# Prelude of a hybrid transformer block: first modulation in column halves, with low-rank products of half the rows between them

## The chip, the cores and the metric

The kernel runs on one core of a Trainium2 chip. A core has five engines with queues of their own: TensorE (PE in the profile, with its weight loads as PEld), VectorE (DVE), ScalarE (ACT), GpSimd (POOL) and SyncE (SP), which here issues most of the DMA transfers. Each engine works through its queue in order, and the engines wait for each other at semaphores. The metric is the device time of one execution in microseconds (us), less is better; the figure of a kernel is the median of its runs.

## The reference

One block with two mixers (attention with a forget gate, and an RWKV-7 recurrence) and a gated convolutional feed-forward layer, in float32, on 1024 rows of width 1024. The change lies at its very start:

```python
mod = silu(c) @ w_mod + b_mod                       # 1024 -> 6 x 1024
shift1, scale1, gate1, shift2, scale2, gate2 = split(mod, 6)
xn  = x * rsqrt(mean(x * x, -1) + 1e-6) * ln1_g
u   = xn * (1 + scale1) + shift1
proj = u @ w_in
...
xw, xa, xg = p_rwkv[..., 1536:]                     # low-rank inputs, widths 64, 64, 128
w_log = -softplus(-(w0 + tanh(xw) @ w2)) - 0.5
a = sigmoid(a0 + xa @ a2)
g = sigmoid(xg) @ g2
```

All products of u are taken in three parts to keep float32 accuracy: u and a weight are each split into a rounded high part and a low part (high = cast, low = value minus high), and high x high, low x high and high x low are added up in PSUM.

## The kernel before

Everything stands in one function, hybrid_block. PE's instructions stand in the order in which the code calls mm; inside the prelude block (lines 413 to 553) the same holds for SP, DVE and ACT, because manual_schedule names these engines. Outside of it, and for GpSimd, a scheduler places instructions, and it may also slip some of the later ones in between those of the prelude.

The prelude holds u transposed: tile kt (0 to 7) has model columns kt x 128 to kt x 128 + 127 on the partitions, and the rows of x, in two halves of 512 (half 0 and 1), along the free dimension. So a modulation value is one number for each partition of a tile: tile kt needs column kt of m1 (shift) and of A1 (ln1_g times 1 + scale). Its steps are these.

- load_x fetches x as eight tiles xt of 128 rows. square (line 425) sums the squares of a tile on ACT, rms_rstd turns them into 1/rms with Ln and Exp, and norm_x (431) puts 1/rms on the diagonal of a matrix dg on DVE.
- turn (466) multiplies four x tiles with these diagonal matrices on PE: the transposed, normalised x lands in a PSUM tile (two buffers), and ACT copies it into uf[half]. There are 16 turns, half 0 first.
- mod_load (438) fetches w_mod for scale (i = 1) or shift (i = 0) as eight tiles of 128 x 1024; the scale's tiles have four buffers (mw), the shift's take those and the slots of x tiles in turns. mod_add (450) adds sc[kt] times such a tile into acc on DVE, eight times. mod_sum (456) adds up acc over its partitions with 128 x 1 products on PE (mps in the profile) and makes m1 and A1 out of them on DVE. The loop at line 532 does this for the scale and then for the shift; warm (445) puts products into PE's queue whose result nobody reads (idle).
- u_steps (472) scales a tile of uf on DVE, casts it to u_hi on ACT and takes u_lo on DVE; half 0, then half 1. low_part (485) multiplies the tile with the two low-rank weight tiles (w_in tiles 24 and 25, raw_in24 and raw_in25; their casts and subtractions are at lines 538 and 545). Three parts, two weights, eight tiles and two halves make 96 products of 128 x 512 (low in the profile).
- low_out (498) moves the four sums out of PSUM. Behind it the first projection products (ps_rkv, weights through load_w, line 256) start; from there on PE works through the projections, the low-rank second products (zp) and all that follows.

Of the kernel before, what the change touches and what calls it, by code (L numbers as in the profile page):

```python
# [132 lines left out]
def hybrid_block(ctx: ExitStack, tc: tile.TileContext, a, out):  # L133
    nc = tc.nc
# [3 lines left out]
    def mm(o, lhsT, rhs, start, stop, more=False):  # L138

        weave.mm_cost(o, lhsT, rhs)  # L140
        nc.tensor.matmul(o, lhsT, rhs, start=start, stop=stop, skip_group_check=more)  # L141
# [24 lines left out]
    def V(name, i=0, n=1):  # L166
        o, _ = VEC[name]
        return vec[:, o + i : o + i + n]
# [6 lines left out]
    ident, ones = f32(eye_r), f32(C("ones"))  # L175
# [16 lines left out]
    sc = cp.tile([128, 8], F32, name="sc")  # L192
# [16 lines left out]
    m2 = cp.tile([128, 16], F32, name="m2")  # L209
# [105 lines left out]
    A1 = cp.tile([128, 8], F32, name="A1")  # L315
    m1 = cp.tile([128, 16], F32, name="m1")
# [3 lines left out]
    u_hi = upool.tile([128, KT, S], F32R, name="u_hi")  # L320
    u_lo = upool.tile([128, KT, S], F32R, name="u_lo")
# [24 lines left out]
    with ExitStack() as es:  # L346
# [65 lines left out]

        with tc.tile_pool(name="st", bufs=1) as st, tc.tile_pool(name="stp", bufs=2, space=PS) as stp, \
                tc.manual_schedule(engines={mybir.EngineType.SP, mybir.EngineType.DVE, mybir.EngineType.Activation}):
            ssq = st.tile([128, 8], F32, name="ssq")
            rstd = st.tile([128, 8], F32, name="rstd")

            def load_x(half):
                xs = []
                for t in range(half * 4, half * 4 + 4):  # L420
                    xs.append(st.tile([128, D], F32, tag="xt", name=f"xt{t}", bufs=8))
                    nc.sync.dma_start(xs[-1], a["x"][t * 128 : t * 128 + 128, :])
                return xs

            def square(half, xs, js):
                for j in js:
                    t = half * 4 + j
                    nc.scalar.activation(uf[1][:, 6:8, :].rearrange("p k s -> p (k s)"), xs[j], AF.Square,
                                         accum_out=ssq[:, t : t + 1])

            def norm_x(half):

                hs = slice(half * 4, half * 4 + 4)
                rms_rstd(rstd[:, hs], ssq[:, hs])
                for j in range(half * 4, half * 4 + 4):
                    ts(dg[:, j, :], ident, rstd[:, j : j + 1], None, op0=ALU.mult)

            def mod_load(i, tags):
                ws = [st.tile([128, D], F32, tag=tags[kt % len(tags)], name=f"wm{i}{kt}", bufs={"mw": 4, "xt": 8}[tags[kt % len(tags)]])
                      for kt in range(KT)]  # L440
                for kt, w in enumerate(ws):
                    nc.sync.dma_start(w, a["w_mod"][kt * 128 : kt * 128 + 128, i * D : i * D + D])
                return ws, st.tile([128, D], F32, name=f"acc{i}")
# [6 lines left out]
            def mod_add(kt, ws, acc):  # L450
                if kt == 0:
                    ts(acc, ws[kt], sc[:, 0:1], None, op0=ALU.mult)
                else:
                    stt(acc, ws[kt], sc[:, kt : kt + 1], acc, op0=ALU.mult, op1=ALU.add)

            def mod_sum(i, acc):
                for j0 in (0, 4):
                    ps = stp.tile([128, 4], F32, tag="mp", name=f"mps{i}{j0}")
                    for j in range(4):
                        c0 = (j0 + j) * 128  # L460
                        mm(ps[:, j : j + 1], acc[:, c0 : c0 + 128], ones[:, 0:1], start=True, stop=True)
                    tt(m1[:, i * 8 + j0 : i * 8 + j0 + 4], ps, V("b_mod", i * 8 + j0, 4), op=ALU.add)
                    if i == 1:
                        stt(A1[:, j0 : j0 + 4], m1[:, 8 + j0 : 12 + j0], 1.0, V("ln1_g", j0, 4), op0=ALU.add, op1=ALU.mult)
# [7 lines left out]
            def u_steps(half):  # L472

                cs = slice(half * NH, half * NH + NH)
                for kt in range(KT + 1):
                    if kt < KT:
                        x = uf[half][:, kt, :]
                        ts(x, x, A1[:, kt : kt + 1], m1[:, kt : kt + 1], op0=ALU.mult, op1=ALU.add)
                        nc.scalar.copy(u_hi[:, kt, cs], x)
                    if kt > 0:  # L480
                        k = kt - 1
                        tt(u_lo[:, k, cs], uf[half][:, k, :], f32(u_hi[:, k, cs]), op=ALU.subtract)
                        yield k

            def low_part(kt, half, parts):
                for (wh, wl), ps in zip(low, low_ps):
                    for i in parts:
                        w, x = ((wh, u_hi), (wh, u_lo), (wl, u_hi))[i]
                        mm(ps[half], w[:, kt * 128 : kt * 128 + 128], x[:, kt, half * NH : half * NH + NH],
                           start=kt == 0 and i == 0, stop=kt == KT - 1 and i == 2)  # L490
# [18 lines left out]

            dg = xwa.rearrange("p (j s) -> p j s", s=128)  # L510
            idle = pb.tile([128, NH], F32, tag="big", name="idle")
            xs = [load_x(half) for half in range(2)]
            m = [mod_load(1, ("mw",)), None]
            uf = [st.tile([128, KT, NH], F32, name=f"uf{half}") for half in range(2)]
            warm(28)
            for half in range(2):
                square(half, xs[half], range(4))
                norm_x(half)
            for half in range(2):
                for kt in range(KT):  # L520
                    nc.scalar.copy(uf[half][:, kt, :], turn(kt, half, xs[half]))
            m[1] = mod_load(0, ("xt", "mw"))
# [6 lines left out]
            nc.sync.dma_start(g2, a["g2"])  # L529
            for o, c0, w in ((0, CST["mask"][0], 128), (128, CST["reset"][0], 256)):  # L530
                nc.sync.dma_start(cst2[:, o : o + w], a["cst"][:, c0 : c0 + w])
            for i in (1, 0):
                for kt in range(KT):
                    mod_add(kt, *m[1 - i])
                mod_sum(i, m[1 - i][1])
                warm((6, 40)[i])
            for raw, hi, _ in low_raw:
                nc.scalar.copy(hi, raw)
            low_ps = [[stp.tile([128, NH], F32, tag=("low", "tp")[hf], name=f"low{j}{hf}") for hf in range(2)] for j in range(2)]
            for half in range(2):  # L540
                for kt in u_steps(half):
                    low_part(kt, half, (0, 1))
                    if half == 0 and kt in (3, 5):
                        raw, hi, lo = low_raw[kt == 5]
                        tt(lo, raw, f32(hi), op=ALU.subtract)
                for kt in range(KT):
                    low_part(kt, half, (2,))
# [691 lines left out]
    ssq = hp.tile([128, 32], F32, name="ssq2")  # L1239
# [74 lines left out]
    for x in range(2):  # L1314
        for n in range(8):
            if x or n:
                k = 8 * x + n + 1
# [332 lines left out]
    ps = wo_do(3, 3)  # L1650
# [7 lines left out]
    ps = wo_do(4, 0)  # L1658
# [15 lines left out]
    for t, k in ((5, 2), (6, 6), (7, 4)):  # L1674
        ps = wo_do(t, k)
# [340 lines left out]
```

## Time and profile before

| what | us |
|---|---|
| median of 3 runs (lowest, highest) | 1667.04 (1666.05, 1668.51) |
| the profiled execution | 1660.79 |
| its span, from the first to the last instruction | 1659.0 |
| first transposing product starts | 14.16 |
| first cast of a low-rank weight on ACT starts | 40.48 |
| first low-rank product starts | 47.58 |
| the two weight subtractions on DVE (128 x 1024) take | 1.22 each |
| DVE busy in the first 64 us | 38.96 |
| ACT busy in the first 64 us | 32.23 |
| GpSimd busy in the first 64 us | 0.92 |

The profile is one execution. Its page gives busy times of the engines, a strip of the span in 40 slices, the chain of waits that ended last, and groups of instructions; the trace behind it can be asked for the instructions of an engine in order of time. A row of such a timeline reads: start, length, engine, line, operation, tile written <- tiles read, shape, count, and in brackets how long the engine had been idle and what released it. Rows can merge several instructions that follow each other. Over the span the DMA engines moved 145 GB/s on average, and between 5 and 20 us as well as between 30 and 40 us about 410 GB/s, which is the most that they reach in this trace.

### The profile page before, as it was taken

What the parts mean: (1) busy time and instruction counts of PE and PEld (TensorE: products, weight loads), DVE (VectorE), ACT (ScalarE), POOL (GpSimd) and SP (SyncE); (2) the same over time, 40 slices, a digit from 0 to 9 for tenths busy, and PEclk for the clock granted to TensorE, in tenths of its full rate; (3) what the DMA queues carried; (4) which work ended last, traced back from release to release, by engine and by line L of the source; (5) the groups of instructions that cost most, each with busy time, mean ns of one, the idle gap of its engine ahead of it and who ended that gap; (6) DMA issues with size and microseconds to landing.
All of it is one profiled execution on the core that took longest, in us unless ns stands there. A gap on an engine that the chain in (4) does not pass through costs nothing.

```text
span 1659.0 us, 25949 instructions
## 1 busy us (share of the span) xinstructions
PE 1613.1 (97%) x9694; PEld 1343.8 (81%) x9694; DVE 1223.7 (74%) x2371; ACT 822.6 (50%) x1540; POOL 128.9 (8%) x152
## 2 busy tenths in 40 slices
PE   8999999999999999999999999999999999999998
PEld 7777778787978778888778887888888888888886
DVE  5786787878876526888678447897777777786677
ACT  5563335445455646766623225654444444555455
POOL 0011101111111010221022000000000000000000
PEclk9999999999999999999999999999999999999999
DMA  9488645443333345433187411233223223574363
GB/s 337 136 325 237 178 117 141 134 121 94 112 107 92 96 133 145 128 110 115 57 322 269 170 74 54 68 136 108 96 95 121 96 97 107 209 266 154 125 210 108
DMA packets 121645, 240.59 MB, mean 145 GB/s; under 512 B 40048, under 2 KB 48880, under 8 KB 121520
## 3 DMA queue, kind: packets, MB, share of 16 engines
q1 hardware_dynamic: 113040, 220.58, 40.8%
q0 software_dynamic: 8480, 18.37, 4.2%
q8 instruction: 76, 1.25, 0.3%
q14 instruction: 49, 0.40, 0.1%
HBM read 173.35 MB, written 65.54 MB: 144 GB/s over the span
## 4 chain that ended last, share of the span: by engine, by line
PE 61%; DVE 4%; DMA 1%; ACT 1%; issue 1%; SPq 0%; DVEq 0%; ACTq 0%
PE X L141 14%; PE D L141 13%; PE Y L141 7%; PE wo L141 5%; PE br L141 5%; PE rk_ps L141 4%; PE gt L141 3%; PE W L141 3%; PE lg L141 2%; PE ov L141 2%; PE tp L145 2%; DMA gg<-d_lora 1%; DVE nm L1050 1%; DVE P L1060 1%; DMA g<-d_gate 0%
## 5 line engine op out<-in xcount | busy, mean ns | idle before, releaser
L141 PE MATMUL D<-op,op 128*128 128x512 f32 x924 | 209.8, 389 | 0.0
L141 PEld LDWEIGHTS D<-op,op 128*128 128x128 f32 x924 | 173.4, 188 | 36.2 <-DVE op L1253 0.3
L141 PE MATMUL X<-T_m,S 128*128 128x512 f32 x440 | 106.9, 389 | 0.0
L141 PEld LDWEIGHTS X<-T_m,S 128*128 128x128 f32 x440 | 82.5, 188 | 17.6 <-ACT x L1543 0.4
L1252 ACT CAST op<-g 128x512 fp32r<-128x512 f32 x77 | 47.8, 621 | 73.5 <-PE D L141 48.3
L1253 DVE TENSOR_TENSOR op<-g,op 128x512 fp32r<-128x512 f32 x77 | 53.0, 689 | 41.2 <-ACT op L1252 41.2
L1503 DVE SCALAR_TENSOR_TENSOR c<-ab,vec,c 128x512 f32<-128x512 f32 x88 | 65.9, 750 | 18.4 <-ACT c L1506 16.9
L784 DVE TENSOR_TENSOR t<-E,M 128x60 f32<-128x60 f32 (+24 forms) x248 | 57.7, 233 | 24.7 <-DMA M<-sm 18.8
L274 DVE TENSOR_TENSOR lo_in<-raw_in,hi_in 128x512 fp32r<-128x512 f32 x84 | 57.8, 726 | 20.9 <-PE gt L141 7.2
L1467 DVE TENSOR_TENSOR A<-ur,A 128x512 fp32r<-128x512 f32 x64 | 44.0, 688 | 39.0 <-ACT A L1463 38.8
L1467 DVE TENSOR_TENSOR S<-ur,S 128x512 fp32r<-128x512 f32 x66 | 45.5, 691 | 35.3 <-ACT S L1463 35.1
L1463 ACT CAST S<-ur 128x512 fp32r<-128x512 f32 x66 | 41.0, 622 | 55.9 <-DVE ur L1456 30.9
L141 PE MATMUL Y<-T_h,S 128*128 128x512 f32 x264 | 65.6, 398 | 1.6 <-ACT T_h L1721 1.0
L141 PE MATMUL Y<-T_h,A 128*128 128x512 f32 x264 | 63.4, 389 | 0.0
L1054 ACT ACTIVATE P<-lg,nm 128x896 f32<-128x896 f32 (+3 forms) x64 | 47.5, 744 | 29.0 <-DVE nm L1050 20.8
L141 PEld LDWEIGHTS Y<-T_h,S 128*128 128x128 f32 x264 | 50.6, 192 | 13.4 <-ACT T_h L1721 1.7
L1463 ACT CAST A<-ur 128x512 fp32r<-128x512 f32 x64 | 39.6, 621 | 42.7 <-PE X L141 29.2
L786 DVE TENSOR_TENSOR E<-E,t 128x60 f32<-128x60 f32 (+24 forms) x248 | 55.9, 225 | 6.6
L141 PE MATMUL W<-B_f,A 128*128 128x512 f32 x252 | 60.6, 389 | 0.0
L141 PE MATMUL X<-B_b,A 128*128 128x512 f32 x252 | 60.5, 389 | 0.0
L141 PEld LDWEIGHTS Y<-T_h,A 128*128 128x128 f32 x264 | 49.5, 188 | 10.3
L272 ACT CAST hi_in<-raw_in 128x1024 fp32r<-128x1024 f32 x42 | 43.8, 1048 | 24.6 <-PE ps_rkv L141 9.4
(481 smaller groups left out, 4135.6 us busy)
## 6 DMA issues: line engine op xcount, KB each, us to landing
raw_in<-in_w_in SPq DMA_DIRECT2D x50, 512.0 KB, 3.8
wm<-in_w_mod SPq DMA_DIRECT2D x48, 512.0 KB, 6.7
ur<-in_w_up SPq DMA_DIRECT2D x44, 512.0 KB, 4.1
g<-d_g SPq DMA_DIRECT2D x35, 512.0 KB, 3.9
d_g<-gs SPq DMA_DIRECT2D x44, 256.0 KB, 2.0
d_g<-c SPq DMA_DIRECT2D x33, 256.0 KB, 4.4
d_st<-qh SPq DMA_DIRECT2D x64, 128.0 KB, 2.5
stA<-d_st POOLq DMA_DIRECT2D x8, 1024.0 KB, 6.5
```

The source lines that it names most:

```text
L141: nc.tensor.matmul(o, lhsT, rhs, start=start, stop=stop, skip_group_check=more)
L145: nc.tensor.transpose(o, i, eye)
L272: nc.scalar.copy(hi, raw)
L274: nc.vector.tensor_tensor(lo[:, c : c + NH], raw[:, c : c + NH], f32(hi[:, c : c + NH]), op=ALU.subtract)
L784: tt(tv, E32[:, 0:J, s : s + 1].to_broadcast([128, J, W]), M32[:, s : s + 1, s + 1 : 32].to_broadcast([128, J, W]), op=ALU.mult)
L786: tt(E32[:, 0:J, s + 1 : 32], E32[:, 0:J, s + 1 : 32], tv, op=ALU.add)
L1054: nc.scalar.activation(e[:, 0:n], lg[:, 0:n], AF.Exp, bias=nm[:, 0:1], accum_out=nm[:, 1:2])
L1252: nc.scalar.copy(hi, src)
L1253: tt(lo, src, f32(hi), op=ALU.subtract)
L1463: nc.scalar.copy(hi, src)
L1467: tt(lo, src, f32(hi), op=ALU.subtract)
L1503: stt(c, ab[:, x + hf * NH : x + hf * NH + NH], V("conv_w", 22 * x + i), c, op0=ALU.mult, op1=ALU.add)
```

## The change

Scale and shift are loaded and summed in column halves: c = 0 holds columns 0 to 511 (u tiles 0 to 3), c = 1 the rest. The order of loads is scale-left, shift-left, the two low-rank weights, scale-right, shift-right, each half as eight tiles of 128 x 512 in ten buffers. u tiles 0 to 3 of both row halves (`first`) are made once the left halves are summed, and their products of the parts high x high and high x low stand between the sums of the right halves; tiles 4 to 7 (`second`) follow. ACT scales all tiles of `first` and half of `second`. The casts and subtractions of the two low-rank weights go from ACT and DVE to GpSimd. Two small tiles of statistics move into m2. Counts of idle products change from 28 + 40 + 6 to 28 + 12 + 6 x 2. The core of the diff:

```diff
-            def mod_load(i, tags):
-                ws = [st.tile([128, D], F32, tag=tags[kt % len(tags)], name=f"wm{i}{kt}", bufs={"mw": 4, "xt": 8}[tags[kt % len(tags)]])
-                      for kt in range(KT)]
...
+            def mod_load(i, c):
+                for kt in range(KT):
+                    w = wm[i, c, kt] = st.tile([128, NH], F32, tag="mw", name=f"wm{i}{c}{kt}", bufs=10)
+                    c0 = i * D + c * NH
+                    nc.sync.dma_start(w, a["w_mod"][kt * 128 : kt * 128 + 128, c0 : c0 + NH])
...
+            def mod_add(i, c, kts):
+                acc = accs1[i][:, c * NH : c * NH + NH]
+                for kt in kts:
+                    if kt == 0:
+                        ts(acc, wm[i, c, kt], sc[:, 0:1], None, op0=ALU.mult)
+                    else:
+                        stt(acc, wm[i, c, kt], sc[:, kt : kt + 1], acc, op0=ALU.mult, op1=ALU.add)
+            def mod_turn(i, c):
+                ps = mps[i, c] = stp.tile([128, 4], F32, tag="mp", name=f"mps{i}{c}")
+                for j in range(4):
+                    c0 = c * NH + j * 128
+                    mm(ps[:, j : j + 1], accs1[i][:, c0 : c0 + 128], ones[:, 0:1], start=True, stop=True)
...
+            def u_scale(half, kt, on_act):
+                x, A, B = uf[half][:, kt, :], A1[:, kt : kt + 1], m1[:, kt : kt + 1]
+                if on_act:
+                    nc.scalar.activation(x, x, AF.Identity, scale=A, bias=B)
+                else:
+                    ts(x, x, A, B, op0=ALU.mult, op1=ALU.add)
+                nc.scalar.copy(u_hi[:, kt, half * NH : half * NH + NH], x)
+            def u_lower(half, kt):
+                cs = slice(half * NH, half * NH + NH)
+                tt(u_lo[:, kt, cs], uf[half][:, kt, :], f32(u_hi[:, kt, cs]), op=ALU.subtract)
+            def low_mm(half, kt, i):
...
             xs = [load_x(half) for half in range(2)]
+            mod_load(1, 0)
+            mod_load(0, 0)
             low_raw = [low_w(24, wp, ("whi", "wlo"), 2), low_w(25, st, ("xt", "xt"), 8)]
             low = [x[1:] for x in low_raw]
+            mod_load(1, 1)
+            mod_load(0, 1)
...
+            warm(28)
+            square(0, xs[0], range(4))
+            norm_x(0)
+            mod_add(1, 0, range(4))
+            pss = [turn(kt, 0, xs[0]) for kt in range(2)]
+            for j in range(4):
+                square(1, xs[1], (j,))
+                if j % 2:
+                    nc.scalar.copy(uf[0][:, j // 2, :], pss[j // 2])
+            norm_x(1)
+            for half, kts in ((0, (2, 3)), (1, range(4)), (0, range(4, KT)), (1, range(4, KT))):
+                for kt in kts:
+                    nc.scalar.copy(uf[half][:, kt, :], turn(kt, half, xs[half]))
+            mod_add(1, 0, range(4, KT))
+            mod_add(0, 0, range(6))
+            mod_turn(1, 0)
+            mod_sum(1, 0)
+            mod_add(0, 0, range(6, KT))
+            warm(12)
+            mod_turn(0, 0)
+            mod_add(1, 1, range(2))
+            mod_sum(0, 0)
+            for raw, hi, lo in low_raw:
+                nc.gpsimd.tensor_copy(hi, raw)
+            for raw, hi, lo in low_raw:
+                nc.gpsimd.tensor_tensor(lo, raw, f32(hi), op=ALU.subtract)
...
+            for n, o in enumerate(first):
+                u_scale(*o, True)
+                if n < 3:
+                    mod_add(1, 1, range(2 + 2 * n, 4 + 2 * n))
+                elif n < 7:
+                    mod_add(0, 1, range(2 * n - 6, 2 * n - 4))
+                if n == 5:
+                    mod_sum(1, 1)
+                low_mm(*o, 0)
+                if n == 3:
+                    mod_turn(1, 1)
+                elif n > 3:
+                    low_mm(*first[n - 4], 2)
+                if n < 6:
+                    warm(2)
+            mod_turn(0, 1)
+            for o in first[4:]:
+                low_mm(*o, 2)
+            for o in first[0:2]:
+                u_lower(*o)
+            mod_sum(0, 1)
+            for n, o in enumerate(second):
+                u_scale(*o, n % 2 == 0)
...
```

GpSimd's queue at the start of the program; hi_in and lo_in are the low-rank weights' high and low parts, w2l and xgs belong to the second low-rank products behind the prelude. Before:

```order
L2005 MEMSET const-uint8-127 128x1
L2012 UNCONDITIONAL_BRANCH
L164 DMA cst<-in_cst 128x384
L562 ISA
L562 TENSOR_TENSOR w2l<-w_343,w2h 128x1024
```

and with the change:

```order
L2058 UNCONDITIONAL_BRANCH
L164 DMA cst<-in_cst 128x384
L554 CAST hi_in_191<-raw_in_189 128x1024
L554 CAST hi_in_195<-raw_in_193 128x1024
L556 ISA
L556 TENSOR_TENSOR lo_in_192<-raw_in_189,hi_in_191 128x1024
L556 TENSOR_TENSOR lo_in_196<-raw_in_193,hi_in_195 128x1024
L608 TENSOR_TENSOR w2l<-w_229,w2h 128x1024
```

Four operations have come ahead of w2l, and the ISA instruction (a reload of GpSimd's code library, which the compiler puts ahead of the first TENSOR_TENSOR) now stands between the casts and the subtractions.

DVE's queue around the first sums, from the diagonals of row half 1 (xwa) on; acc_138 is the scale's sum, acc_137 the shift's, wm are the w_mod tiles, and every row is a half-width tile. With the change:

```order
L435 TENSOR_SCALAR xwa<-cst,m_98 128x128 x4
L454 SCALAR_TENSOR_TENSOR acc_138<-wm_165,sc,acc_138 128x512
...
L454 SCALAR_TENSOR_TENSOR acc_137<-wm_183,sc,acc_137 128x512
L464 TENSOR_TENSOR m_103<-mps_395,vec 128x4
L466 SCALAR_TENSOR_TENSOR A_102<-m_103,vec 128x4
L454 SCALAR_TENSOR_TENSOR acc_137<-wm_185,sc,acc_137 128x512
L454 SCALAR_TENSOR_TENSOR acc_137<-wm_187,sc,acc_137 128x512
L452 TENSOR_SCALAR acc_138<-wm_197,sc 128x512
L454 SCALAR_TENSOR_TENSOR acc_138<-wm_199,sc,acc_138 128x512
L464 TENSOR_TENSOR m_103<-mps_416,vec 128x4
L454 SCALAR_TENSOR_TENSOR acc_138<-wm_201,sc,acc_138 128x512
```

The scale-left sum (m from mps_395) is taken with two shift-left additions still behind it, and the shift-left sum (mps_416) behind two additions of scale-right. The eight rows that "..." leaves out are additions of the same form.

ACT's queue at the end of the `first` tiles; uf_140 and uf_139 are row halves 1 and 0, raw_in_667 is the first projection weight. With the change:

```order
L478 ACTIVATE uf_140<-uf_140,m_103,A_102 128x512
L481 CAST u_hi<-uf_140 128x512
L478 ACTIVATE uf_140<-uf_140,m_103,A_102 128x512
L272 CAST hi_in_669<-raw_in_667 128x1024
L481 CAST u_hi<-uf_140 128x512
L478 ACTIVATE uf_139<-uf_139,m_103,A_102 128x512
L481 CAST u_hi<-uf_139 128x512 x2
```

Before, the cast of that weight stood behind the second u tile of row half 1, with the casts of six tiles behind it:

```order
L538 CAST hi_in_341<-raw_in_339 128x1024
L479 CAST u_hi<-uf_172 128x512 x8
L479 CAST u_hi<-uf_173 128x512 x2
L272 CAST hi_in_645<-raw_in_643 128x1024
L479 CAST u_hi<-uf_173 128x512 x6
```

It has moved between the scaling of the eighth `first` tile and that tile's cast. On SP the load of this weight stands behind all modulation loads, the four of w2, g2 and the two of cst2, in both kernels.

More of the change, by code (lines that the diff above doesn't have):

```diff
@@ L448, in warm, with mod_sum @@
                     mm(idle[:, 0:NC1], cst[:, 0:128], cst, start=True, stop=True)
[L450 to L464, printed above, removed]
+            def mod_add(i, c, kts):
[10 more added lines that the diff above has]
+                    mm(ps[:, j : j + 1], accs1[i][:, c0 : c0 + 128], ones[:, 0:1], start=True, stop=True)
+            def mod_sum(i, c):
+                j0 = c * 4
+                tt(m1[:, i * 8 + j0 : i * 8 + j0 + 4], mps[i, c], V("b_mod", i * 8 + j0, 4), op=ALU.add)
+                if i == 1:
+                    stt(A1[:, j0 : j0 + 4], m1[:, 8 + j0 : 12 + j0], 1.0, V("ln1_g", j0, 4), op0=ALU.add, op1=ALU.mult)
             def turn(kt, half, xs):
@@ L511, in hybrid_block @@
             idle = pb.tile([128, NH], F32, tag="big", name="idle")
+            wm, mps, low_n = {}, {}, {}
+            accs1 = {i: st.tile([128, D], F32, name=f"acc{i}") for i in range(2)}
+            uf = [st.tile([128, KT, NH], F32, name=f"uf{half}") for half in range(2)]
             xs = [load_x(half) for half in range(2)]
[L513 to L522, printed above, removed]
+            mod_load(1, 0)
+            mod_load(0, 0)
             low_raw = [low_w(24, wp, ("whi", "wlo"), 2), low_w(25, st, ("xt", "xt"), 8)]
             low = [x[1:] for x in low_raw]
+            mod_load(1, 1)
+            mod_load(0, 1)
             w2 = rp.tile([128, S], F32, tag="raw", name="w2")
@@ new lines, in hybrid_block @@
+            first, second = ([(half, kt) for half in range(2) for kt in kts] for kts in (range(4), range(4, KT)))
+            for n, o in enumerate(first):
[13 more added lines that the diff above has]
+                    warm(2)
@@ L548, in hybrid_block @@
+            u_lower(*second[-1])
+            for o in second[-2:]:
+                low_mm(*o, 1)
             nc.scalar.copy(w2h, w2)
```

49 lines of the change are left out of this document (14 added, 35 removed).

## Prediction

> **What bounds the kernel now.** I read the page's busy shares first, then the chain of waits, then the timeline of the first 110 us engine by engine, because the diff touches nothing behind the low-rank products.
>
> ```profile
> PE 1613.1 (97%) x9694; PEld 1343.8 (81%) x9694; DVE 1223.7 (74%) x2371; ACT 822.6 (50%) x1540; POOL 128.9 (8%) x152
> ```
>
> TensorE (PE) has work for 97% of the span, so after the prelude a microsecond is only won by starting the same PE queue earlier. What the prelude is worth is the moment at which the first projection product (ps_rkv) starts. The timeline of PE (start and length in us from the span's start), and then that of DVE:
>
> ```profile
> 14.16 1.95 PE L141 MATMUL tr<-xwa,xt 128*128 128x128 f32 x16
> 17.07 13.06 PE L141 MATMUL tr<-xwa,xt 128*128 128x128 f32 x112 [0.96 <-ACT uf L521]
> 30.22 1.95 PE L141 MATMUL mps<-cst,acc 128*128 128x1 f32 x16
> 42.62 3.04 PE L141 MATMUL mps<-cst,acc 128*128 128x1 f32 x16 [1.83 <-DVE acc L454]
> 58.10 3.88 PE L141 MATMUL low<-u_hi,lo_in 128*128 128x512 f32 x16
> 61.82 0.40 PE L141 MATMUL low<-u_hi,hi_in 128*128 128x512 f32 x1
> 73.37 1.99 PE L141 MATMUL ps_rkv<-u_hi,hi_in 128*128 128x512 f32 x8
> ```
>
> ```profile
> 31.31 0.16 DVE L462 TENSOR_TENSOR m<-mps,vec 128x4 f32<-128x4 f32 x1 [1.15 <-PE mps L141]
> 31.51 0.16 DVE L464 SCALAR_TENSOR_TENSOR A<-m,vec 128x4 f32<-128x4 f32 x1
> 33.26 9.21 DVE L454 SCALAR_TENSOR_TENSOR acc<-wm,sc,acc 128x1024 f32<-128x1024 f32 x7
> 45.77 1.00 DVE L478 TENSOR_SCALAR uf<-uf,A,m 128x512 f32<-128x512 f32 x2
> ```
>
> PE transposes x until 30.13. Then VectorE (DVE) sums the shift's weights over all 1024 columns until 42.47 while PE runs only idle fillers; u begins at 45.77, and the 96 low-rank products end at 73.37. Sixteen of them take 61.82 - 58.10 = 3.72 us, 0.2325 each, so 96 need 22.3 of those 27.6 us. The target is thus the 15 us between the last transpose and the first u.
>
> **The change, part by part.** I follow what ends last in the new order; scale is part 1, shift part 0, left the columns 0 to 511.
>
> *Transposes.* A turn of four transposes has eight PE records of 13.06/112 = 0.1166, so 0.933 us. The order now puts ScalarE's (ACT) copy of turn 1 ahead of the last two squares and that of turn 2 behind them:
>
> ```profile
> 13.65 1.06 ACT L428 ACTIVATE uf<-xt 128x1024 f32<-128x1024 f32 x1
> 14.83 1.06 ACT L428 ACTIVATE uf<-xt 128x1024 f32<-128x1024 f32 x1
> 16.01 0.30 ACT L298 ACTIVATE rstd<-ssq,epsr 128x4 f32<-128x4 f32 x1
> 16.34 0.20 ACT L299 ACTIVATE rstd<-rstd 128x4 f32<-128x4 f32 x1
> ```
>
> ACT is free at 13.65 but turn 1 ends at 14.16 + 0.93 = 15.1. Copy to 15.7, two squares at 1.18 to 18.1, copy to 18.7, Ln and Exp to 19.2. The fourth turn needs the second copy, the fifth the third copy (19.9). Twelve turns from 19.9 end at 31.1, one microsecond later than now. The left sums need no more than that: four half-width sums precede the second diagonals, and ten more at 0.78 each (below) end near 28.
>
> *First left half.* From mps to the finished scale took 31.67 - 30.22 = 1.45 us, so 32.5. VectorE has two half-width sums left before shift-left.
>
> ```profile
> L1503 DVE SCALAR_TENSOR_TENSOR c<-ab,vec,c 128x512 f32<-128x512 f32 x88 | 65.9, 750 | 18.4 <-ACT c L1506 16.9
> L266 POOL CAST hi_in<-raw_in 128x1024 fp32r<-128x1024 f32 x6 | 6.2, 1037 | 31.0 <-issue 19.8 <-PE gt L141 7.4 <-PE rk_ps L141 3.8
> L562 POOL TENSOR_TENSOR w2l<-w,w2h 128x1024 fp32r<-128x1024 f32 x1 | 2.4, 2409 | 67.0 <-PE low L141 67.0
> 103.89 2.37 POOL L575 TENSOR_TENSOR xgs<-xg,xgs 128x1024 fp32r<-128x1024 f32 x1 [9.28 <-ACT xgs L574]
> 106.22 2.27 POOL L572 TENSOR_TENSOR g2s<-g,g2s 128x512 fp32r<-128x512 f32 x1
> ```
>
> ```profile
> 105.20 2.14 DVE L222 SCALAR_TENSOR_TENSOR acc<-wm,sc,acc 128x1024 f32<-128x1024 f32 x1 [0.77 <-DMA wm<-in_w_mod]
> 107.74 1.83 DVE L222 SCALAR_TENSOR_TENSOR acc<-wm,sc,acc 128x1024 f32<-128x1024 f32 x1 [0.40 <-DMA wm<-in_w_mod]
> ```
>
> A half-width sum is 0.66 (half of 9.21/7) to 0.75 by the row; each waits for the one before, so I take 0.78. GpSimd (POOL) matters here. The last four rows, of POOL and DVE, take turns: the sum that began at 105.20 ends 1.08 after xgs ends, the next 1.08 after g2s ends. A two-input DVE sum stands still while POOL subtracts. POOL's second cast writes over x tiles that the row-half-0 transposes read until 19.9 + 8 x 0.933 = 27.4, so cast 1.04 and two subtractions of 2.41 end at 33.2. The two sums run 33.2 to 34.8, their turn takes 1.1, shift-left is ready at 36.1. The order has an ISA instruction, a reload of POOL's code library, between its casts and subtractions. The trace has no price for it: nothing from below, from above anything within the 67 us that POOL was idle before w2l. I take nothing and keep the other end as a rival.
>
> *Eight u tiles on ACT* with sixteen main and eight cross products plus fillers between them.
>
> ```profile
> L1378 ACT ACTIVATE u_m<-tr,m,A 128x512 f32<-128x512 f32 x8 | 5.6, 782 | 0.0
> L479 ACT CAST u_hi<-uf 128x512 fp32r<-128x512 f32 x16 | 9.6, 619 | 12.7 <-DVE uf L478 12.7
> ```
>
> 0.78 + 0.62 = 1.40 us a tile, the eighth would be ready at 47.3. But in ACT's queue the cast of the first projection weight stands between the eighth tile's scale and its cast, and that weight is loaded last:
>
> ```profile
> 52.08 2.48 SPq L528 DMA_DIRECT2D w<-in_w2a  x4
> 54.60 0.58 SPq L529 DMA_DIRECT2D g<-in_g  x1
> 55.23 0.91 SPq L531 DMA_DIRECT2D cst<-in_cst  x2
> 56.24 7.23 SPq L260 DMA_DIRECT2D raw_in<-in_w_in  x2
> 60.69 1.05 ACT L272 CAST hi_in<-raw_in 128x1024 fp32r<-128x1024 f32 x1 [1.97 <-DMA raw_in<-in_w_in]
> ```
>
> SP's last shift-right load waits for the buffer of the sixth scale-right sum: four sums from 36.1, 39.3, issue to 39.7. Then the seven small loads, 56.24 - 52.08 = 4.16, to 43.8; landing 60.69 - 56.24 = 4.45, to 48.3; cast to 49.3, eighth u tile 49.9. Behind it on PE stand four products (0.93) and the turn of shift-right (1.1): 51.9. All other sums are done by then (last at 47.3).
>
> *Rest.* Then PE has 8 + 64 products: 72 x 0.2325 = 16.7, end at 68.6. ACT (eight casts and four scales, 8 x 0.62 + 4 x 0.78 = 8.1) and DVE (twenty operations of at most 0.75, 15.0) stay ahead of that.
>
> *Clock.* PE runs dry from about 46.9 to 49.9. These rows (busy PE, PEld, DVE, ACT, POOL, then the granted clock) and two products show what that can cost:
>
> ```profile
> 33.00:34.00 1.00, 1.00 (x5) 1.00 (x5) 0.96 (x2) 0.00 (x0) 0.00 (x0) 0.50 1.00 401
> 43.00:44.00 1.00, 1.00 (x7) 1.00 (x7) 0.02 (x1) 0.00 (x0) 0.00 (x0) 0.59 0.05 16
> 50.00:51.00 1.00, 1.00 (x5) 0.80 (x5) 1.00 (x3) 0.62 (x1) 0.00 (x0) 1.00 0.00 0
> ```
>
> ```profile
> 48.01 0.63 PE L141 MATMUL low<-u_lo,hi_in 128*128 128x512 f32 x1
> 48.43 0.63 PE L141 MATMUL low<-u_hi,hi_in 128*128 128x512 f32 x1
> ```
>
> The clock falls at 43.4 (0.59 over that microsecond) and is whole again from 50.0, 6.6 us or two equal steps of 3.3 later; after 1.83 us of idling and a turn that uses PE little it stood at half, a product taking 0.42. One such step costs 3.3 x (1 - 0.2325/0.42) = 1.5 us if all of it meets products, nothing if none does. Part of it will lie in the idling, so I take 0.9: the end at 69.5, bounds 68.6 and 70.1. [...]
>
> *What costs nothing.*
>
> ```profile
> L442 SPq DMA_DIRECT2D wm<-in_w_mod x16: 327/328/1418, 5.5 to 30.2; - x16
> 80.26 1.04 ACT L272 CAST hi_in<-raw_in 128x1024 fp32r<-128x1024 f32 x1
> 84.26 1.98 PE L141 MATMUL ps_rkv<-u_hi,hi_in 128*128 128x512 f32 x8
> ```
>
> Sixteen loads more on SP at 0.33 us: the queue waits for buffers there, and they move as many bytes; without that cover 5.3 us. The two statistics tiles moved into m2 change no instruction. Fewer DVE scales and weight subtractions free an engine that no longer ends last. Behind ps_rkv PE's order is the same; the third projection weight may come late, since the second load queued ahead of it now waits for the low products. It was cast at 80.26, 4.0 us ahead of its use at 84.26; landing behind 1.5 MB more could eat that and, by one landing of 4.45, about 2 us beyond. I take nothing.
>
> *Sum.* 69.5 - 73.37 = -3.9 us. The profiled execution took 1660.79 us (span 1659.0), so 1656.9 there; it lies 6.25 below the median of the runs, 1667.04, and carried to that the forecast is 1663.1.
>
> **The rivals.**
>
> *GpSimd collides with the sums (slower).* If its subtractions begin only when shift-left is summed, about 34.6, instead of 28.4, the first (to 37.0) holds up the second scale-right sum and so the sum of shift-left, to 37.8; the second starts there and holds the next sum to 40.2. The sixth scale-right sum ends at 40.2 + 4 x 0.78 = 43.3 instead of 39.3, and SP, the weight, the eighth tile and PE follow it: 68.6 + 4.0 = 72.6. PE then idles 5 to 7 us and meets a whole step at half rate: 74.1, or +0.7, 1667.8; with another among the transposes (below) 75.7, 1669.4. It decides once GpSimd's start is some 4 to 11 us late. For it speaks the reload between casts and subtractions, which stood ahead of everything before; against it, that no row of the trace shows it taking time. [...] Chance 0.32.
>
> *The weight is not last.* If it lands before the eighth tile, that tile is ready at 47.3, the turn ends at 49.3 and PE at 49.3 + 16.7 = 66.0, without idling: -7.4, 1659.6. Against it: seven issues and 4.45 us of landing would have to shrink. Chance 0.08.
>
> *Half clock among the transposes.* PE now waits for ACT's copy from 17.0 to 18.7 and again to 19.9. Before, 0.96 us there left the clock whole, 1.83 us later on did not. A step of 3.3 us at half adds half of it, 1.6, to all behind it: 71.1, -2.3, 1664.8. Chance 0.07.
>
> *Given back behind.* The start moves, but the third weight or VectorE is late by the 2 us above, or more: 1665 to 1668. Chance 0.05.
>
> **How the numbers follow.** The forecast has 0.48. A measurement of this kernel can tell about 0.2%, 3.3 us, from no change. The forecast's own range, 1661 to 1665.5, has about four fifths of its weight beyond that: faster 0.38 + 0.08 = 0.46. No change: 0.10 of the forecast, 0.07, about 0.02 of the last rival and nearly half of the collision, 0.145: 0.34. Slower: the rest of the collision and of the last, 0.20. The range takes in both the early weight and the collision with the half clock: 1659 to 1670.
>
> **What would show it.** In the changed profile: transposes ending near 31; the first u tile on ACT near 36; ACT idle ahead of the first projection weight's cast, until about 48; ps_rkv starting near 69.5. Wrong is the GpSimd step if its first subtraction starts after 34 or sums of 512 columns take 2 us; wrong is the weight step if ACT does not wait there; wrong is the clock step if it stays whole past 50; and wrong is the whole carrying-over if ps_rkv starts 4 us earlier and the span does not shrink by it.

## The result and the profile after

| what | before | after |
|---|---|---|
| median of 12 runs, us | 1663.19 | 1665.87 |
| lowest, highest | 1659.19, 1668.51 | 1659.89, 1668.20 |
| the profiled execution (span) | 1660.79 (1659.0) | 1662.62 (1660.9) |
| ps_rkv starts, in that execution | 73.37 | 73.30 |

The ratio is 1.0011, with a 95% interval of 1.0000 to 1.0022: no change that can be told from none, where 3.9 us less was forecast. That 1665.87 lies inside the stated range of 1659 to 1670 is no success: the range was wide, and the kernel before, whose three runs had a median of 1667.04, has 1663.19 here. The changed kernel's page and the timeline of its PE (start, length, what; in brackets the idle time ahead and its releaser) show why: the products are spread differently, but the first projection product starts where it did.

```profile
PE 1608.2 (97%) x9672; PEld 1340.6 (81%) x9672; DVE 1221.6 (74%) x2373; ACT 828.9 (50%) x1550; POOL 135.6 (8%) x156
```

```profile
29.96 0.95 PE L141 MATMUL mps<-cst,acc 128*128 128x1 f32 x8
...
36.06 1.05 PE L141 MATMUL mps<-cst,acc 128*128 128x1 f32 x8 [2.92 <-DVE acc L454]
38.96 1.19 PE L141 MATMUL low<-u_hi,hi_in 128*128 128x512 f32 x2 [1.84 <-ACT u_hi L481]
...
51.88 1.22 PE L141 MATMUL low<-u_hi,hi_in 128*128 128x512 f32 x2 [2.30 <-ACT u_hi L481]
...
53.75 1.70 PE L141 MATMUL mps<-cst,acc 128*128 128x1 f32 x8
55.31 3.60 PE L141 MATMUL low<-u_hi,lo_in 128*128 128x512 f32 x8
...
73.30 1.98 PE L141 MATMUL ps_rkv<-u_hi,hi_in 128*128 128x512 f32 x8
```

Low-rank products now start at 38.96 instead of 47.58. But PE stands idle for 2.30 us ahead of 51.88, and the eight cross products from 55.31 take 3.60 us, about twice 8 x 0.2325. Who released PE at 51.88 is seen in the timelines of ACT, then SP, then POOL and DVE:

```profile
37.35 0.81 ACT L478 ACTIVATE uf<-uf,m,A 128x512 f32<-128x512 f32 x1 [6.60 <-DVE m L464]
...
46.93 0.81 ACT L478 ACTIVATE uf<-uf,m,A 128x512 f32<-128x512 f32 x1
50.26 1.04 ACT L272 CAST hi_in<-raw_in 128x1024 fp32r<-128x1024 f32 x1 [2.51 <-DMA raw_in<-in_w_in]
51.21 0.61 ACT L481 CAST u_hi<-uf 128x512 fp32r<-128x512 f32 x1
```

```profile
40.80 2.48 SPq L527 DMA_DIRECT2D w<-in_w2a  x4
...
45.14 8.29 SPq L260 DMA_DIRECT2D raw_in<-in_w_in  x2
```

```profile
28.90 1.04 POOL L554 CAST hi_in<-raw_in 128x1024 fp32r<-128x1024 f32 x1 [0.31 <-DMA raw_in<-in_w_in]
29.99 4.68 POOL L556 TENSOR_TENSOR lo_in<-raw_in,hi_in 128x1024 fp32r<-128x1024 f32 x2
```

```profile
31.15 1.23 DVE L466 SCALAR_TENSOR_TENSOR A<-m,vec 128x4 f32<-128x4 f32 x1
32.30 3.71 DVE L454 SCALAR_TENSOR_TENSOR acc<-wm,sc,acc 128x512 f32<-128x512 f32 x2
```

The eighth u tile is scaled at 46.93, but its cast (51.21) waits in ACT's queue behind the cast of the first projection weight, which lands at 50.26. DVE's A, 0.16 us of work, takes 1.23, and two sums that need 1.53 (in the run without GpSimd, below) take 3.71: until 34.67 they stand while POOL subtracts.

What comes behind ps_rkv is the same. The gate product f of the attention starts 31.5 us behind ps_rkv in each kernel (before: 31.60, after: 31.46):

```profile
104.97 2.04 PE L141 MATMUL f<-u_hi,wf 128*40 128x512 f32 x8 [0.83 <-ACT z L599]
```

```profile
104.76 2.04 PE L141 MATMUL f<-u_hi,wf 128*40 128x512 f32 x8 [0.82 <-ACT z L645]
```

So the 1.9 us by which the two spans differ arise later, where PE has the same 9364 products in the same order in both kernels; the twelve runs of the kernel before lie up to 9.3 us apart.

### The profile page after: what moved, and what is told of

Read it like the earlier page. It is cut to its first block, busy times and chain, and to the rows that moved or that the text cites. A ratio compares the mean times of both kernels' runs of the same rounds, so it can differ in the third digit from the quotient of the medians.

```text
span 1660.9 us, 25962 instructions
## 1 busy us (share of the span) xinstructions
PE 1608.2 (97%) x9672; PEld 1340.6 (81%) x9672; DVE 1221.6 (74%) x2373; ACT 828.9 (50%) x1550; POOL 135.6 (8%) x156
## 4 chain that ended last, share of the span: by engine, by line
PE 61%; DVE 4%; ACT 2%; DMA 2%; issue 1%; SPq 0%; DVEq 0%; ACTq 0%
PE X L141 14%; PE D L141 13%; PE Y L141 7%; PE wo L141 5%; PE br L141 5%; PE rk_ps L141 3%; PE W L141 3%; PE gt L141 3%; PE lg L141 2%; PE ov L141 2%; PE tp L145 2%; DMA d_gate<-gs 1%; DVE nm L1096 1%; DVE P L1106 1%; DMA g<-d_gate 0%
## 5 line engine op out<-in xcount | busy, mean ns | idle before, releaser
L1549 DVE SCALAR_TENSOR_TENSOR c<-ab,vec,c 128x512 f32<-128x512 f32 x88 | 65.9, 750 | 18.4 <-ACT c L1552 16.9
```

The lines of the kernel that those rows point to most:

```text
L1549: stt(c, ab[:, x + hf * NH : x + hf * NH + NH], V("conv_w", 22 * x + i), c, op0=ALU.mult, op1=ALU.add)
```

## The experiments

The theory ("gate"): the start of ps_rkv is set by the eighth u tile, whose cast waits behind the weight's, and by the half clock that this idling brings. Rivals: GpSimd's hold on DVE is the loss ("GpSimd"); the shift-right sums end last anyway ("sums"); the clock costs little. In all runs ratios are to the kernel before, on the same chip, with their 95% intervals. The start of ps_rkv comes from one profiled execution of each; two of the changed kernel differ by 0.90 us (last experiment), so that smaller differences at ps_rkv decide nothing by themselves.

**One cast behind another.** The scheduler put the weight's cast ahead of the eighth tile's; a dependency turns the two round, and nothing else on any engine.

```diff
-            nc.scalar.copy(hi, raw)
+            i = nc.scalar.copy(hi, raw)
+            if name == "in16":
+                tc.add_manual_dep(i.ins, marks["u"].ins.name, NOSYNC)
...
-                nc.scalar.copy(u_hi[:, kt, half * NH : half * NH + NH], x)
+                i = nc.scalar.copy(u_hi[:, kt, half * NH : half * NH + NH], x)
+                if (half, kt) == (1, 3):
+                    marks["u"] = i
```

> The changed kernel with one instruction moved: on ScalarE the cast of the first projection weight stands behind the cast of the eighth u tile instead of ahead of it. Theory 'gate' (that wait, and the clock that falls in the idling it causes, hold the start of ps_rkv at 73.3): eighth u tile ready at 48.3 instead of 51.8, TensorE not idle ahead of it, granted clock whole from 45 on, the shift-right turn done near 51.5; then VectorE still waits for the weight cast (51.3) before its subtraction, so the last modulation comes at 52.8 and the ninth tile at 54.4, a stall of 0.6; ps_rkv at 68.5 (68 to 69.5), 4.8 us earlier, time against the kernel before 0.997. Rival 'sums' (the shift-right sums or their loads end last anyway): ps_rkv at 72 to 73.5, TensorE idle ahead of the shift-right turn. Rival 'GpSimd' (its lock on VectorE costs the start 3 us, the rest little): ps_rkv at 72 or later.

ps_rkv 69.27, time 0.9974 (0.9955 to 0.9993). ACT, DVE and PE of this run:

```profile
48.45 0.62 ACT L483 CAST u_hi<-uf 128x512 fp32r<-128x512 f32 x1
51.07 1.05 ACT L272 CAST hi_in<-raw_in 128x1024 fp32r<-128x1024 f32 x1 [2.00 <-DMA raw_in<-in_w_in]
```

```profile
52.15 1.29 DVE L276 TENSOR_TENSOR lo_in<-raw_in,hi_in 128x512 fp32r<-128x512 f32 x2 [2.32 <-ACT hi_in L272]
53.36 0.15 DVE L466 TENSOR_TENSOR m<-mps,vec 128x4 f32<-128x4 f32 x1
```

```profile
55.07 0.72 PE L141 MATMUL low<-u_hi,hi_in 128*128 128x512 f32 x2 [0.91 <-ACT u_hi L483]
69.27 1.98 PE L141 MATMUL ps_rkv<-u_hi,hi_in 128*128 128x512 f32 x8
```

The weight comes no earlier, yet one instruction moved wins 4.0 us: "sums" and "GpSimd" fall, as both wanted 72 or later. The rest of the wait is seen as forecast: the last addition m (53.36) stands behind the weight's subtraction on DVE, which costs PE 0.91. That 69.27 is close to the forecast of 69.5 is chance: in the forecast the weight's cast still stands ahead of the eighth tile's.

**GpSimd taken out.** Casts of the low-rank weights on ACT behind the last transpose's copy, subtractions on DVE behind the eighth scale-right sum, the weight's cast kept where the change has it.

```diff
-                nc.gpsimd.tensor_copy(hi, raw)
-            for raw, hi, lo in low_raw:
-                nc.gpsimd.tensor_tensor(lo, raw, f32(hi), op=ALU.subtract)
+                nc.scalar.copy(hi, raw)
...
+                if n == 2:
+                    for raw, hi, lo in low_raw:
+                        tt(lo, raw, f32(hi), op=ALU.subtract)
```

> The changed kernel with the two low-rank weights' casts on ScalarE behind the last transpose's copy and their subtractions on VectorE behind the eighth scale-right sum; GpSimd has neither. The queues are otherwise the same, the eighth u tile's cast still stands behind the weight's. Theory 'gate': scale-left ready at 31.4 (A in 0.16 instead of 1.23 us), shift-left summed at 32.9, first u tile on ScalarE at 34.4 instead of 37.35, first projection weight issued at 42.1 instead of 45.14, eighth u tile at 48.9 instead of 51.8, TensorE still idle ahead of it and its clock at half for 6.8 us there: ps_rkv near 70.3 (69.5 to 71.2), time against the kernel before 0.998 to 0.999. Rival 'GpSimd' (its lock is the whole loss): ps_rkv at 69.5 or earlier. Rival 'sums': VectorE carries 2.44 us more, so ps_rkv at 73 or later.

ps_rkv 73.52, time 1.0018 (1.0002 to 1.0034). ACT, PE, and a row of what SP's queue waited for (us, times, longest):

```profile
34.40 0.82 ACT L480 ACTIVATE uf<-uf,m,A 128x512 f32<-128x512 f32 x1 [1.51 <-DVE m L466]
50.03 1.04 ACT L487 CAST hi_in<-raw_in 128x1024 fp32r<-128x1024 f32 x1 [5.22 <-DMA raw_in<-in_w_in]
```

```profile
51.65 1.22 PE L141 MATMUL low<-u_hi,hi_in 128*128 128x512 f32 x2 [6.18 <-ACT u_hi L490]
73.52 1.98 PE L141 MATMUL ps_rkv<-u_hi,hi_in 128*128 128x512 f32 x8
```

```profile
SPq L536 <- DVE lo_in L574: 2.3, 1, 2.3
```

The first u tile comes at 34.40, 3 us earlier, as expected, and nothing is won (the time is 0.02 to 0.34% longer): PE only idles 6.18 us instead of 2.30. That GpSimd's hold is the whole loss is refuted, since the run before won 4.0 us with the hold in place. My 70.3 missed too: the small load w2 takes the buffer of the first low-rank weight, which the later subtraction frees late, so SP waits 2.3 us and the projection weight still lands at 50.0. The edit moved the gate's cause instead of removing it.

**The idling filled.** Eleven idle products ahead of the eighth tile's; then the same and fourteen more ahead of the shift-left turn; then eighteen alone.

```diff
+                if n == 7:
+                    warm(11)
                 low_mm(*o, 0)
```

> The changed kernel with eleven idle products (128 x 384, about 0.2 us each) more on TensorE ahead of the eighth u tile's products, to cover the 2.3 us in which it idles there. Theory 'gate': the eighth tile comes at 51.8 as before, the granted clock stays whole past 51.8, the four products, the turn and the eight cross products behind it take 3.8 instead of 6.9 us; ps_rkv at 70.3 (69.6 to 71), time against the kernel before 0.998 to 0.999. Rival 'clock costs little' (u tiles or sums would not have been ready earlier): ps_rkv at 72.5 to 73.5.

> As the run with eleven idle products ahead of the eighth u tile, and fourteen more ahead of the shift-left turn, where TensorE idles for 2.9 us and the clock then is at half from 38.1 to 45.0. Theory 'gate': between 38 and 46 ScalarE's 1.37 us a tile sets the pace and TensorE at half clock (1.5 us a tile) lags by a microsecond at most, which the wait for the eighth tile takes up; the clock is whole throughout, ps_rkv at 70.3, within 0.5 of the run with only the second filling. Rival 'the first half clock counts too': ps_rkv a microsecond or more ahead of that run.

> The changed kernel with eighteen idle products ahead of the eighth u tile's products instead of the eleven that ended 1.16 us too early (ps_rkv 72.31, one window of 3.4 us at half clock left). Theory: the clock is set by windows of 3.41 us in which TensorE worked or not, and 1.16 us of idling with the turn of 0.95 in one of them was enough; with no idling the clock stays whole from 45 on, the eighth tile's products start near 52.6, ps_rkv at 70.9 (70.3 to 71.6), time against the kernel before 0.998 to 0.9995. Rival (the turn alone lowers the clock, or tiles are late): 72 or later.

ps_rkv 72.31, 72.36 and 71.75; times 0.9994 (0.9981 to 1.0007), 0.9991 (0.9979 to 1.0003), 0.9984 (0.9970 to 0.9998). PE of the first, and of the third, then a window of the first and one of the second (us, then length, busy PE, PEld, DVE, ACT, POOL, the granted clock, share and GB/s of the DMA engines):

```profile
52.44 0.73 PE L141 MATMUL low<-u_hi,hi_in 128*128 128x512 f32 x2 [1.16 <-ACT u_hi L481]
53.01 0.62 PE L141 MATMUL low<-u_hi,lo_in 128*128 128x512 f32 x2
53.47 0.95 PE L141 MATMUL mps<-cst,acc 128*128 128x1 f32 x8
54.28 3.58 PE L141 MATMUL low<-u_hi,lo_in 128*128 128x512 f32 x8
```

```profile
53.56 0.62 PE L141 MATMUL low<-u_hi,hi_in 128*128 128x512 f32 x2
...
55.29 2.11 PE L141 MATMUL low<-u_hi,lo_in 128*128 128x512 f32 x8
```

```profile
51.07:54.48 3.41, 2.25 (x15) 1.87 (x14) 1.32 (x3) 1.31 (x2) 0.00 (x0) 1.00 0.01 2
```

```profile
40.40:43.81 3.41, 3.41 (x9) 2.86 (x10) 3.27 (x6) 3.31 (x6) 0.00 (x0) 0.50 0.94 316
```

Eleven fillers ended 1.16 us too early, and the clock fell once more, for half as long: my 70.3 was too low. Eighteen kept it whole there. From the eighth tile's products to ps_rkv it is 21.42 us in the changed kernel (73.30 - 51.88), 19.87 with eleven and 18.19 with eighteen: the half clock there costs 3.2 us. The gain at ps_rkv is smaller, and 71.75 lies just behind the expected range, since in the third run the shift-left turn met a half clock too (1.87 us), the u tiles came 1.2 later, and the fillers held TensorE for 0.5 beyond the eighth tile (ready at 53.07, its products from 53.56). Filling the first gap as well changed ps_rkv by 0.05. The clock was not whole there, as I had expected: the fillers shortened its half from 6.8 us (38.13 to 44.96) to 3.4 (40.40 to 43.81). ACT sets the pace in that stretch, a tile each 1.37 us without a gap, and TensorE still idled ahead of the eighth tile in both runs (1.16 and 1.64 us). So the half clock before 45 costs nothing that counts.

**GpSimd alone in the kernel before.** A dependency, not shown, keeps the first projection weight's cast at its place in ACT's queue.

```diff
-                nc.scalar.copy(hi, raw)
+                nc.gpsimd.tensor_copy(hi, raw)
+            for raw, hi, lo in low_raw:
+                nc.gpsimd.tensor_tensor(lo, raw, f32(hi), op=ALU.subtract)
...
-                    if half == 0 and kt in (3, 5):
-                        raw, hi, lo = low_raw[kt == 5]
-                        tt(lo, raw, f32(hi), op=ALU.subtract)
```

> The kernel before with one part of the change alone: the casts and subtractions of the two low-rank weights on GpSimd, all other queues as they were. Theory 'lock': GpSimd subtracts from about 42.7 to 47.4; the last modulation's addition on VectorE, at 45.69 in the kernel before, waits for it until about 47.4, u begins 1.7 us later, and VectorE's 2.44 us of subtractions saved behind it give back the 1.3 us that TensorE idled there: ps_rkv at 73.4 to 74.6 against 73.37, time 1.000 to 1.001. Rival 'free engine' (GpSimd works beside VectorE): u begins at 45.8, ps_rkv at 72.0 to 72.4, time 0.999.

ps_rkv 74.38, time 1.0007 (0.9990 to 1.0023). POOL and DVE:

```profile
39.87 3.94 POOL L542 CAST hi_in<-raw_in 128x1024 fp32r<-128x1024 f32 x2 [37.90 <-DMA raw_in<-in_w_in]
43.86 4.67 POOL L544 TENSOR_TENSOR lo_in<-raw_in,hi_in 128x1024 fp32r<-128x1024 f32 x2
```

```profile
46.64 0.16 DVE L464 TENSOR_TENSOR m<-mps,vec 128x4 f32<-128x4 f32 x1 [1.54 <-PE mps L141]
46.72 2.55 DVE L480 TENSOR_SCALAR uf<-uf,A,m 128x512 f32<-128x512 f32 x2
```

1.0 us later, in the expected range, but at another instruction than I named: the addition m, which reads PSUM, passes in 0.16 beside POOL; the first u scale behind it stands until POOL ends at 48.53 (two scales 2.55 instead of 1.00). And POOL's two casts, 1.04 each when DVE is idle, take 3.94 beside DVE's sums: the hold works both ways. The 1.0 us is not the price of the hold alone: the granted clock was at half from 41.03 to 54.69 here, and from 43.17 to 50.00 in the kernel before.

**Towards a better version.** First, the weight cast last and its load issued ahead of the seven small ones. Then the same with the low-rank subtractions on DVE behind the shift-left sums and six fillers. Then these subtractions one place later, behind the addition m that the first u tile needs, the weight's subtraction behind the last m, no fillers. The diff shows the early load alone.

```diff
+            early["in16"] = rp.tile([128, D], F32, tag="raw", name="raw_in16")
+            nc.sync.dma_start(early["in16"], a["w_in"][16])
             w2 = rp.tile([128, S], F32, tag="raw", name="w2")
```

> The changed kernel with the first projection weight cast behind the eighth u tile (as in the run that gave 69.27) and its load issued ahead of the seven small loads instead of behind them. Theory 'gate': weight issued near 41 instead of 45.6 and landed before the eighth tile is cast, so VectorE's subtraction for it is done before the last modulation, which comes right behind the shift-right turn (near 51.8 instead of 53.4); the ninth tile's stall of 0.9 on TensorE is gone: ps_rkv at 68.2 (67.6 to 68.9), time against the kernel before 0.997. Rival 'sums' (VectorE's own work holds the last modulation): ps_rkv stays at 69.3.

> The same, and the two low-rank weights' casts on ScalarE, their subtractions on VectorE right behind the shift-left sums, nothing of them on GpSimd; six idle products more ahead of the shift-right turn. Theory 'gate' with 'lock' (GpSimd's subtractions hold VectorE for their whole length, but behind the weight's wait that cost nothing; with that wait gone it does): first u tile on ScalarE near 34.5 instead of 37.4 to 38, eighth ready at 45.5; the right sums end where they do now, near 47.5, and set the shift-right turn (48.6); the last modulation waits for the first weight's subtraction, 50.2; ps_rkv at 65.9 (65 to 67), time against the kernel before 0.9955. Rival 'lock costs nothing': ps_rkv within 0.5 of the run with GpSimd, 68.2.

> The changed kernel with the first projection weight loaded early and cast behind the eighth u tile (as in the run that gave 67.25), the low-rank weights' casts on ScalarE, their subtractions on VectorE behind the shift-left addition (not ahead of it, where they held the first u tile back to 36.29), the first weight's subtraction behind the last modulation's addition, and no idle products ahead of the shift-right turn. Theory 'gate' with 'lock': first u tile on ScalarE at 34.4, eighth ready at 45.5, right sums done at 46.9, shift-right turn done at 47.9, no stall behind it; ps_rkv at 64.4 (63.9 to 66), time against the kernel before 0.9945 to 0.996. Rival 'PE or ScalarE sets it': ps_rkv not below 66.

| run | ps_rkv | time (95% interval) |
|---|---|---|
| early, cast last | 67.25 | 0.9972 (0.9961 to 0.9984) |
| the same, no GpSimd | 66.72 | 0.9974 (0.9961 to 0.9988) |
| the last one | 65.33 | 0.9959 (0.9946 to 0.9972) |

The first came 0.35 us ahead of its expected range: the weight was issued at 40.93 and m came at 50.96 right behind the turn; the stall went, and the clock stayed whole from 45 on. The second came at 66.72 instead of 65.9, inside its range, and its time missed the expected 0.9955: DVE works in order, and the two subtractions stood ahead of m, so the first u tile came at 36.29 instead of 34.5; the six fillers held the turn for 1.05 us more. In the last one DVE and ACT read:

```profile
34.75 0.16 DVE L470 TENSOR_TENSOR m<-mps,vec 128x4 f32<-128x4 f32 x1
34.83 2.36 DVE L566 TENSOR_TENSOR lo_in<-raw_in,hi_in 128x1024 fp32r<-128x1024 f32 x2
```

```profile
34.95 0.81 ACT L484 ACTIVATE uf<-uf,m,A 128x512 f32<-128x512 f32 x1 [1.49 <-DVE m L470]
```

```profile
96.77 2.06 PE L141 MATMUL f<-u_hi,wf 128*40 128x512 f32 x8 [0.82 <-ACT z L655]
```

ps_rkv at 65.33 lies 8.0 us ahead of the kernel before, f (96.77) 8.2 ahead of it, and the time is 0.41% less, 6.8 us (4.7 to 9.0): the start carries over, as far as the interval tells. Between the first and the last of these times the intervals do not decide. The median of the last is 1656.05 against 1663.47, the lowest of all kernels tried.

**The changed kernel once more.**

> The changed kernel itself, unaltered, for a second profile and a narrower interval. Theory 'no gain at the start, nothing lost behind it': ps_rkv within 1 of 73.3 and time against the kernel before 0.9995 to 1.0005. Rival 'something is lost behind ps_rkv as well': the same ps_rkv and time 1.001 or more.

ps_rkv 74.20, time 1.0007 (0.9995 to 1.0019). PE idled 3.10 us ahead of the eighth tile there, and the clock fell as in the first profile. The shift-left turn met a half clock (1.86 us instead of 1.05), so that the first u tile came at 38.55 instead of 37.35 and what follows came late too. Whether something under 0.2% is lost behind ps_rkv the two intervals leave open; the profiles show no place for it. PE has the same 9364 products there in the same order in all kernels, and from ps_rkv to the end of the span they take 1587.6 us in the first profile of the changed kernel, 1591.9 in this one and 1585.6 in the kernel before.

## Why the prediction was wrong

It forecast ps_rkv at 69.5; it came at 73.30. The mechanism was named (the weight's cast ahead of the eighth tile, then a half clock). What failed are two terms of the sum, which were too small: *Clock*, taken at 0.9 us, cost 3.2, and the weight's path to the eighth tile ended 1.9 us later than summed. A third was slightly off the other way.

- *Transposes*: forecast to end at 31.1, ended at 30.1 (the turn begins at 29.96). No effect: DVE's next sums waited for POOL anyway.
- *First left half.* Shift-left was to be summed at 34.8 and was at 36.0. I let POOL's second cast wait for the x tiles' buffer (27.4); it waited for its own load, until 28.90. And I charged the hold only to the sums, where A stood behind the first subtraction already. The late end of 1.2 us is that start.
- *The weight, +1.9.* The sixth scale-right sum ended about 1.0 later for the same reason, the weight was issued at 45.14 instead of 43.8, and it took 5.12 us to land instead of 4.45: the eighth tile was ready at 51.8 instead of 49.9. The experiment with one cast moved shows that this wait decides; it takes away the wait and the half clock behind it together, 4.0 us.
- *Clock, +2.3.* I read one step of 3.3 us at half, priced it between 0 and 1.5 and took 0.9, since part would meet idling. It cost 3.2, by the runs with fillers: the clock fell as the eighth tile's products began and stayed down for 6.8 us, two steps, nearly all of them with work. By the prediction's own sign, that the clock must not stay whole past 50, the step was wrong: it was whole until 51.78.
- *Products and turn, -0.5*: the stretch from the eighth tile to ps_rkv takes 18.19 us at the whole clock (with eighteen fillers), where the forecast had 18.7 (49.9 to 68.6) without the loss.

1.9 + 2.3 - 0.5 = 3.7 of the 3.8 us between 69.5 and 73.30, and so nearly all of the 3.9 that were forecast. *What costs nothing* held: the third weight was no wait, and where the start came earlier the time fell with it. The interval allows the full amount in all these runs but one, in which ps_rkv came 6.7 us earlier (66.72) and the time is 4.3 less (2.0 to 6.5). Of the rivals, *GpSimd collides* named an engine that does hold DVE, but not the price: its subtractions began at 29.99, not at 34.6. The reload of POOL's library that stood for it took no visible time; 0.05 us lie between the second cast's end (28.90 + 1.04) and the first subtraction, and the two subtractions take 4.68, no more than twice the 2.41 of the kernel before. *The weight is not last* was the right picture of what the change lacked: with it made true, and the cast behind the eighth tile's, ps_rkv came at 67.25.

## What to carry to other kernels

When work is split so that a later stage can start in the middle of an earlier one, look at what a scheduler has slipped in between in each in-order queue: here one cast for a later stage, harmless behind ten tiles in the old order, became the gate at the eighth. Removing a wait ahead of such a gate only lengthens the idling at it (3.0 us won on the first tile, 3.9 us more idle), so find the last release before tuning the first. Moving two-input work from VectorE to GpSimd was no relief while VectorE was busy with the same kind of work (two sums took 3.71 us beside GpSimd's subtractions, 1.53 without), and where TensorE had to wait 2.30 us, the half clock behind it cost more than the wait, 3.2 us.

## What the runs showed of the hardware

In the profiles of the two kernels the granted clock changes only on a grid of 3.41 us (in the changed kernel at 38.13, 44.96, 51.78, 58.61 and 225.87: 2, 2, 2 and 49 steps apart; in the kernel before at 32.93, 36.34, 43.17 and 50.00: 1, 2 and 2 steps apart). Where the grid lies differs from one execution to the next: in the repeat of the changed kernel the clock changes at 36.15, 42.98, 53.22 and 60.05, and the shift-left turn met it otherwise (1.86 us there, 1.05 in the first profile). In windows cut on this grid, the changed kernel shows (us, then length, busy PE, PEld, DVE, ACT, POOL, then the granted clock, share and GB/s of the DMA engines):

```profile
31.30:34.72 3.42, 1.84 (x11) 1.52 (x9) 3.42 (x2) 0.00 (x0) 3.37 (x2) 1.00 0.40 147
34.72:38.13 3.41, 1.05 (x8) 0.97 (x8) 3.30 (x7) 0.78 (x1) 0.00 (x0) 1.00 0.50 144
38.13:41.54 3.41, 2.58 (x7) 2.23 (x8) 3.27 (x5) 3.31 (x7) 0.00 (x0) 0.50 0.91 296
41.54:44.96 3.42, 3.42 (x13) 3.03 (x11) 3.28 (x6) 3.36 (x6) 0.00 (x0) 0.50 1.02 311
44.96:48.37 3.41, 3.41 (x20) 3.06 (x21) 3.31 (x7) 2.72 (x5) 0.00 (x0) 1.00 0.93 270
48.37:51.78 3.41, 1.21 (x6) 0.69 (x4) 1.25 (x3) 1.52 (x2) 0.00 (x0) 1.00 0.11 44
51.78:55.20 3.42, 3.32 (x12) 2.94 (x12) 0.85 (x2) 0.04 (x1) 0.00 (x0) 0.50 0.28 74
55.20:58.61 3.41, 3.41 (x10) 2.73 (x10) 3.12 (x7) 2.86 (x5) 0.00 (x0) 0.50 0.62 235
58.61:62.02 3.41, 3.41 (x17) 2.79 (x16) 3.41 (x7) 2.39 (x4) 0.00 (x0) 1.00 0.00 0
```

The window with 1.84 us of products left the clock whole; the one with 1.21 was followed by half. At half clock the window with 3.42 was followed by the whole clock, the one with 2.58 was not. In the run with eleven fillers the window with 2.25 us of work, 0.95 of it a turn, was followed by half, so a window need not be idle for that. A turn of 128 x 1 products seems to count for little: the window from 34.72 holds 1.05 us of it and nothing else, and the clock falls; that from 51.78 is busy for 3.32, 1.45 of them in a turn, and the clock stays at half. So it is in the kernel before, where a turn fills 30.22 to 32.03 of the first of these windows, 1.81 us, and the second is at half:

```profile
29.52:32.93 3.41, 3.32 (x27) 3.13 (x26) 1.66 (x6) 0.92 (x2) 0.00 (x0) 1.00 1.02 406
32.93:36.34 3.41, 3.41 (x13) 3.41 (x12) 3.30 (x4) 0.00 (x0) 0.00 (x0) 0.50 1.02 412
```

Beside a subtraction on POOL, sums, A and the scaling of u stood still: in the changed kernel two sums took 3.71 us and A 1.23, where the run without GpSimd has 1.53 and 0.16; with GpSimd alone in the kernel before, two scales took 2.55 instead of 1.00. The addition m, with one input in PSUM, took its 0.16 beside POOL there. That the input in PSUM is the reason is my reading; no run tells it from others.
